# Score pieces on two PSUM banks, the state's sum in one round, and moved splits, in a block of recurrent and attention layers

## The chip, the cores and the metric

The kernel runs on one core of one Trainium2 chip. The metric is the device time of one execution in microseconds (us). PE is TensorE (matmuls, with its weight loads in the row PEld), DVE is VectorE, ACT is ScalarE, POOL is GpSimd, SP is SyncE, whose queue issues nearly every DMA of this kernel.

## The reference

The input goes through a first block (a gated delta rule, a dilated attention, a feed-forward stage), which the change does not touch, and through two layers of a second block, over 1,280 tokens (256 of context and 1,024 others). Each layer of the second block computes, cut to what matters here:

```python
proj = h @ w_in                                # ..., queries, keys, values, gates
# a linear recurrence in both directions over chunks of 64 tokens, 6 heads of 64:
#   state' = decay * (state + what the chunk adds, itself a function of state)
ys = rwkv_bidir(...)
# attention, 6 query heads on 2 key heads, each query over all 1280 keys
s  = q @ k.T ;  p = softmax(s) ;  ya = p @ v
# neighbourhood attention, 4 heads: 8 or 9 rows of 64 keys, with a bias, and the 256 of context
yn = softmax(concat(q @ k_nb.T + bias, q @ k_ctx.T)) @ v
x  = layer_norm(ALPHA * x + gate * (concat(ys, ya, yn) * gates) @ w_out)
```

## The kernel before

A layer of the second block has three stages. In the **projections** (`project`, `project_rest`) the columns of `w_in2` are loaded by `Dense.load` in slabs of 256: each half slab of 128 columns is a DMA into `wraw`, then `split` makes an fp32r high part on ACT (`whi`, L148) and a low part as the difference (`wlo`, L149; POOL unless another engine is named). A product is three matmuls for each of eight slices of the inner dimension (L208 to L210). `Dense.chan` keeps the weights stationary and streams up to 512 tokens. `Dense.tok` keeps 128 tokens stationary and streams the weights' columns. Two places for `whi` and `wlo` take turns, so a slab waits for the matmuls of the slab before last.

Values are 384 columns: for each of ten token tiles one `tok` of 256 columns and one of 128 into the same bank, a copy to `nv` and a DMA. These loads stand at the end of `project_rest`, behind `qk_norm`, whose ten tiles PE, DVE, ACT and POOL work on together with `factors`, the recurrence's inputs.

The **rounds** follow: attention and recurrence, recorded in an order written out by `Rounds`. Every piece of work is a generator that yields a phase and a lag. A round runs through its phases in the order of `PHASES`, and in each phase through all generators that wait for it and whose lag is over. B and Q exist only in odd rounds. The order of recording is the order of instructions on PE, DVE, ACT and POOL; SP's order is left to the framework's scheduler. Per round there is at most:

- scores: a piece of up to 512 columns, as a pair of matmuls (L648) into tag "a", which is one PSUM bank. DVE adds the bias, writes `S` and takes the maximum (L652). Of four pieces three have phase F0 of a round each, and the fourth F2 of the third one's round. When a row of 1,280, 768, 832 or 256 columns is complete, `soft` has ACT take the exponential (L607) and DVE the reciprocal.
- values: one group of four transposes (F1, L684) into tag "t", an ACT copy to `PT` (L688), and the products of the group before (V, L703). Four buffers `S` bound how far scores run ahead.
- the scan of the recurrence: for each of ten block pairs and two chunks, `pw` (L1726), an ACT copy to `W`, `pw` again (L1740), an ACT copy to `SA`, then `py` (L1749, closed by L1767) for the output and `pc` (L1732, closed by L1755) for the new state, which two DVE operations (L1763) scale into `SK`. The chunk takes four rounds.
- `prep`: products and a triangular inverse (`tri_inverse2`) for each of 30 triples, three at a time. It sends a small matrix to DRAM and reads it back spread over partitions (`wR<-wD`), then does 30 small POOL operations (L396, L398).
- `end`: the normalisation of a finished group, and the DMA of `y` to `ydr` (L1818).

Layer 1 computes no output for the context, and so has fewer attention jobs. In `finish`, last, each token tile is read back from `ydr`, gated, multiplied by `w_out` and normalised. Its pools and the recurrence's lie on the same side of SBUF.

Of the kernel before, what the change touches and what calls it, by code (L numbers as in the profile page):

```python
# [27 lines left out]
FIRST = {**ATT, "mm": FULL[0], "r": FULL[0], "o": FULL[1], "g": FULL[5], "h": [(6, 0, 256), (6, 256, 512)],  # L28
         "s": FULL[7]}
SECOND = {**ATT, "mm": FULL[0], "g": FULL[5], "h": [(6, 0, 256), (5, 0, 256), (6, 0, 256), (5, 256, 512)],  # L30
          "z": [(6, 256, 384), (6, 384, 512)], "s": [(7, 0, 384)], "c": [(1, 0, 384)]}


class Consts:
# [139 lines left out]
class Dense:  # L174
# [3 lines left out]
    def __init__(self, k, pools, rpool, width=256, raws=1):  # L178
        self.k, self.pools, self.rpool, self.width, self.raws, self.turn = k, pools, rpool, width, raws, 0

    def load(self, segs, kt=8, width=None, pool=None):

        width = width or self.width
        nc = self.k.nc
        i = "" if pool else self.turn % len(self.pools)
        if not pool:
            self.turn += 1
            pool = self.pools[i]
        hi = pool.tile([128, kt, width], F32R, tag=f"whi{i}", name="whi", bufs=1)
        lo = pool.tile([128, kt, width], F32R, tag=f"wlo{i}", name="wlo", bufs=1)  # L190
        for ap, c0 in segs:
            n = ap.shape[1]
            rw = min(128, width) if kt == 8 else width // 2
            for a in range(0, n, rw):
                m = min(rw, n - a)
                raw = self.rpool.tile([128, kt, rw], F32, tag="wraw", name="wraw", bufs=self.raws)[:, :, :m]
                nc.sync.dma_start(raw, ap[:, a:a + m].rearrange("(k p) n -> p k n", p=128))
                c = slice(c0 + a, c0 + a + m)
                self.k.split(hi[:, :, c], lo[:, :, c], raw)
        return hi, lo  # L200

    def product(self, p, lhs, rhs):
# [159 lines left out]
def tri_inverse2(k, pool, At, out, ticket):  # L362

    nc = k.nc
# [21 lines left out]
    x = new("X16", (128, 4, 16))  # L386
    nc.gpsimd.tensor_copy(x, k.c("eye16")[:, None, :].to_broadcast([128, 4, 16]))
    tmp = new("Y16", (128, 4, 16))
    yield "-", 3
    for i in range(15):  # L390
        if i in (3, 6, 10):
            yield "-", 1
# [191 lines left out]
def attend_rounds(k, rounds, wk, jobs, width, bufs):  # L584
# [18 lines left out]
        state.more = False  # L603

    def soft(s, mx, total, job):
        yield "-", 1
        nc.scalar.activation(s[:, :total], s[:, :total], AF.Exp, bias=mx[:, 5:6], accum_out=mx[:, 6:7])  # L607
        yield "-", 1
        nc.vector.reciprocal(mx[:, 7:8], mx[:, 6:7])
        job[2].append((s, mx))  # L610
        if len(job[2]) == 2:
            ready.append(job)

    def scores():
        count = 0
        while state.more or loaded:
            if not loaded:
                yield "-", 1
                continue
            segs, blocks, out = loaded.pop(0)  # L620
            job = [blocks, out, []]
            total = sum(n for n, _, _ in segs)
            for h in range(2):
                while live[0] >= bufs:
                    yield "-", 1
                live[0] += 1
                s = wk.tile([128, width], F32, tag="S", name="S", bufs=bufs)
                mx = wk.tile([128, 8], F32, tag="mx", name="mx", bufs=8)

                pieces, c0 = [], 0  # L630
                for n0, score, bias in segs:
                    a = 0
                    while a < n0:
                        n = min(n0 - a, 512 - c0 % 512)
                        if c0 % 512 == 0:
                            pieces.append([])
                        pieces[-1].append((c0, a, n, score, bias))
                        a += n
                        c0 += n
                j = 0  # L640
                for piece in pieces:
                    count += 1
                    yield ("F2", 0) if count % 4 == 0 else ("F0", 1)
                    p = k.bank([128, 512], "a")
                    for c0, a, n, score, bias in piece:
                        ops = score(h, a, n)
                        for i, (lhsT, rhs) in enumerate(ops):
                            nc.tensor.matmul(p[:, c0 % 512:c0 % 512 + n], lhsT=lhsT, rhs=rhs, start=i == 0,  # L648
                                             stop=i == len(ops) - 1)
                    for c0, a, n, score, bias in piece:  # L650
                        b = bias(h)[:, a:a + n] if bias is not None else k.zero.to_broadcast([128, n])
                        nc.vector.tensor_tensor_reduce(out=s[:, c0:c0 + n], in0=p[:, c0 % 512:c0 % 512 + n], in1=b, scale=1.0,  # L652
                                                       scalar=-3.0e38, op0=ALU.add, op1=ALU.max, accum_out=mx[:, j:j + 1])
                        j += 1
                if j > 1:
                    nc.vector.tensor_reduce(mx[:, 5:6], mx[:, :j], AX.X, ALU.max, negate=True)  # L656
                else:
                    nc.vector.tensor_scalar(mx[:, 5:6], mx[:, 0:1], -1.0, None, ALU.mult)
                rounds.add(soft(s, mx, total, job))
            state.scored += 1  # L660

# [744 lines left out]
def project_rest(k, I, l, last, hp, dn, hT, L):  # L1406
# [24 lines left out]
        next(side, None)  # L1431
        next(side, None)

    wq = [dn.load([(W[:, 1280 + g * 256:1536 + g * 256], 0)]) for g in range(2)]
    for t in range(10):
        p = k.bank([128, 512], "mm")
        for g in range(2):
# [1 line left out]
        qk_norm(k, hp, p, t, last, L)  # L1439
        next(side, None)  # L1440
        next(side, None)
    wv = [dn.load([(W[:, 1792:2048], 0)]), dn.load([(W[:, 2048:2176], 0)])]
    for t in range(10):
        p = k.bank([128, 512], "mm")[:, :384]
        dn.tok(wv[0], 0, 256, hT, t * 128, p=p[:, :256])
        dn.tok(wv[1], 0, 128, hT, t * 128, p=p[:, 256:])
        nv = hp.tile([128, 384], F32, tag="nv", name="nv", bufs=2)
        k.copy(nv, p)
        nc.sync.dma_start(L.nv[:, t], nv)
        next(side, None)  # L1450
    for _ in side:
        pass

# [134 lines left out]
class Rounds:  # L1588
# [1 line left out]

    PHASES = (("-", "F0", "F1", "F2", "V"), ("-", "F0", "F1", "F2", "V", "B", "Q"))

    def __init__(self):
        self.live, self.r = [], 0
# [27 lines left out]
def rwkv(k, rounds, wk, l, last, L):  # L1624
# [86 lines left out]
    def scan():  # L1711
        for s in range(10):
# [6 lines left out]
            for ci in range(2):  # L1719
# [4 lines left out]
                for pr, d, u in units:  # L1724
                    for h in range(2):
                        nc.tensor.matmul(pw[HS[h], pr, d], lhsT=g[h][:, pr, u, 0:64], rhs=sk[h][:, pr, 0, u],  # L1726
                                         start=True, stop=True)
                if new:
                    pc = k.bank([128, 3, 2, 64], "c")
                    for pr, d, u in units:  # L1730
                        for h in range(2):
                            nc.tensor.matmul(pc[HS[h], pr, d], lhsT=sk[h][:, pr, 1, u], rhs=sk[h][:, pr, 0, u],  # L1732
                                             start=(pr, d) == (0, 0), stop=False, skip_group_check=True)
                W = t1("W", (128, 3, 2, 64))
                nc.scalar.copy(W, pw)
                yield "B", 1
# [4 lines left out]
                                         start=True, stop=True)  # L1741
                SA = t1("SA", (128, 3, 2, 64), 2)
                nc.scalar.activation(SA, pw, AF.Copy, scale=-1.0)
                yield "V", 1
                if want(s):
                    py = k.bank([128, 3, 2, 64], "s")
                    for pr, d, u in units:
                        for h in range(2):
                            nc.tensor.matmul(py[HS[h], pr, d], lhsT=sk[h][:, pr, 0, u], rhs=g[h][:, pr, u, 64:128],  # L1749
                                             start=(pr, d) == (0, 0), stop=False, skip_group_check=True)  # L1750
                yield "B", 0
                if new:
# [36 lines left out]
    def end(o, pr, g):  # L1789
# [17 lines left out]
        nc.vector.tensor_copy(rs, pm)  # L1807
        yield "-", 1
        k.rsqrt(rs, rs, 1.0 / 64, 64e-5)
        yield "V", 1  # L1810
        pm = k.bank([128, 2, 128], "mm")
        for b in range(2):
            for h in range(2):
# [417 lines left out]
```

## Time and profile before

| | us |
|---|---|
| median of 2 runs | 4754.6 |
| the two runs | 4746.42, 4762.78 |
| the profiled execution | 4747.42 |
| its span, first to last instruction | 4745.4 |
| layer 0's rounds, about | 2235 to 3065 |
| layer 1's rounds, about | 3815 to 4650 |

The granted clock has the mean 0.904 over the span; 1.0 stands for 2.4 GHz and 0.5 for 1.2 GHz. A matmul's row includes its passage through the array, so rows of one run overlap, and what PE can do in a stretch is read from the distance of starts. A wait is PE's idle time in front of an instruction, put down to what released it.

### The profile page before, as it was taken

Reading aid. Unit: us, or ns where it says so; the run is one execution under the profiler, and the core shown is the slowest. Engines: PE = TensorE matmul, PEld = TensorE weight load, DVE = VectorE, ACT = ScalarE, POOL = GpSimd, SP = SyncE. Lnnn points to the kernel's source line nnn. Section 1 sums busy time; section 2 is a strip of 40 time slices with the busy share of each in tenths; the row PEclk is TensorE's granted clock in tenths of the full one; section 3 lists DMA queues with packets and bytes.
Section 4 is the critical chain, followed back from the end, with each engine's and each line's share of the span. In section 5 each row is a group of like instructions: output and inputs, shape, how many; then the busy total and the mean of one; then the engine's idle time right before and its main releaser. Section 6 shows DMA issues by size and latency. Waiting matters only on the chain. (4 is left out here: it accounts for less than half of the span.)

```text
span 4745.4 us, 92034 instructions
## 1 busy us (share of the span) xinstructions
PE 4060.8 (86%) x37134; PEld 3294.0 (69%) x37134; DVE 2142.5 (45%) x4637; ACT 1479.2 (31%) x2843; POOL 1861.8 (39%) x3279
## 2 busy tenths in 40 slices
PE   8999998989999898985778887788988758887888
PEld 6767778777888687775556666567877736666667
DVE  5533333693121543561344444455446334444445
ACT  4244443311111312321334433332133124433342
POOL 2433343432222524562243443235257332434423
PEclk9999999999999899987879987789998868988889
DMA  3433224452111324533222223433355232223343
GB/s 108 135 114 90 82 81 140 147 160 67 45 49 45 120 86 127 199 116 92 56 71 63 68 73 80 126 104 109 106 181 174 80 96 53 68 63 81 83 116 123
DMA packets 525403, 472.01 MB, mean 99 GB/s; under 512 B 67344, under 2 KB 447792, under 8 KB 524848
## 3 DMA queue, kind: packets, MB, share of 16 engines
q1 hardware_dynamic: 524976, 466.13, 33.2%
q8 instruction: 291, 4.77, 0.4%
q14 instruction: 136, 1.11, 0.1%
HBM read 335.54 MB, written 130.43 MB: 98 GB/s over the span
## 5 line engine op out<-in xcount | busy, mean ns | idle before, releaser
L149 POOL TENSOR_TENSOR wlo<-wraw,whi 128x1024 fp32r<-128x1024 f32 (+3 forms) x188 | 451.5, 2414 | 737.4 <-ACT whi L148 647.3
L396 POOL TENSOR_TENSOR wY<-wR,wX 128x60 f32<-128x60 f32 (+1 forms) x900 | 229.2, 255 | 385.5 <-DMA wR<-wD 324.2
L652 DVE CUSTOM_DVE_ANT_0 S<-bank,zero 128x256 f32<-128x256 f32 (+1 forms) x372 | 208.2, 560 | 289.4 <-PE bank L648 287.8
L148 ACT CAST whi<-wraw 128x1024 fp32r<-128x1024 f32 (+3 forms) x188 | 182.8, 999 | 470.1 <-PE bank L209 172.1
L688 ACT COPY PT<-bank 128x512 f32<-128x512 f32 x346 | 202.2, 585 | 347.9 <-PE bank L684 346.0
L210 PE MATMUL bank<-h2T,wlo 128*128 128x512 f32 x704 | 278.3, 397 | 0.0
L209 PE MATMUL bank<-h2T,whi 128*128 128x512 f32 x704 | 277.9, 395 | 0.0
L208 PE MATMUL bank<-h2T,whi 128*128 128x512 f32 x704 | 275.7, 394 | 0.3 <-ACT h2T L744 0.3
L684 PE MATMUL bank<-cst,S 128*128 128x128 f32 (+1 forms) x1416 | 255.2, 308 | 21.6 <-ACT PT L688 15.0
L398 POOL TENSOR_TENSOR wX<-wX,wY 128x60 f32<-128x60 f32 (+1 forms) x900 | 238.2, 265 | 70.5
L703 PE MATMUL bank<-PT,nav 128*64 128x128 f32 (+1 forms) x2832 | 260.8, 309 | 4.3 <-ACT PT L688 3.4
L607 ACT ACTIVATE S<-S,mx 128x1280 f32<-128x1280 f32 (+3 forms) x180 | 202.9, 1127 | 189.0 <-DVE mx L656 183.5
L208 PE MATMUL bank<-whi,yh 128*128 128x256 f32 x832 | 242.6, 292 | 18.4 <-ACT yh L148 14.3
L210 PE MATMUL bank<-whi,yl 128*128 128x256 f32 x832 | 240.4, 289 | 1.9 <-DVE yl L149 1.9
L209 PE MATMUL bank<-wlo,yh 128*128 128x256 f32 x832 | 241.3, 290 | 0.0
L684 PEld LDWEIGHTS bank<-cst,S 128*128 128x128 f32 (+1 forms) x1416 | 180.3, 155 | 70.1 <-ACT PT L688 36.7
L703 PEld LDWEIGHTS bank<-PT,nav 128*64 128x64 f32 (+1 forms) x2832 | 164.7, 149 | 79.6 <-issue 66.5
L208 PE MATMUL bank<-hA,whi 128*128 128x512 f32 (+1 forms) x528 | 197.1, 373 | 25.4 <-ACT fo L126 14.9
L648 PE MATMUL bank<-k1h,qst 128*128 128x512 f32 (+2 forms) x234 | 121.2, 520 | 104.7 <-DVE mx L652 103.3
L375 POOL TENSOR_TENSOR wB<-A,cst 128x256 f32<-128x256 f32 x60 | 44.8, 747 | 407.5 <-DVE A L1687 396.9
L208 PE MATMUL bank<-hT,whi 128*128 128x512 f32 x464 | 189.8, 409 | 9.6 <-ACT sqkv L126 6.7
L209 PE MATMUL bank<-hA,whi 128*128 128x512 f32 (+1 forms) x528 | 196.2, 372 | 0.4 <-POOL hA L149 0.4
(447 smaller groups left out, 11176.3 us busy)
## 6 DMA issues: line engine op xcount, KB each, us to landing
wraw<-in_w_in SPq DMA_DIRECT2D x86, 512.0 KB
wR<-wD SPq DMA_DIRECT2D x60, 512.0 KB
wm<-in_w_mod SPq DMA_DIRECT2D x96, 256.0 KB
X<-R SPq DMA_DIRECT2D x12, 1280.0 KB
G<-gt SPq DMA_DIRECT2D x24, 640.0 KB
bk<-bk SPq DMA_DIRECT2D x24, 640.0 KB
bk<-bk SPq DMA_DIRECT2D x120, 128.0 KB
G<-G SPq DMA_DIRECT2D x240, 64.0 KB
```

Source lines behind the costliest of these rows:

```text
L148: self.nc.scalar.copy(hi, raw)
L149: (eng or self.nc.gpsimd).tensor_tensor(lo, raw, hi.bitcast(F32), ALU.subtract)
L208: nc.tensor.matmul(p, lhsT=lh, rhs=rh, start=kk == 0, stop=False)
L209: nc.tensor.matmul(p, lhsT=lh, rhs=rl, start=False, stop=False)
L210: nc.tensor.matmul(p, lhsT=ll, rhs=rh, start=False, stop=kk == n - 1)
L396: nc.gpsimd.tensor_tensor(t, custom(R, i * 64 + i + 1, [((15 - 2 * i) * 64 + 31 - i, 2), (16, 2), (1, n)]), custom(x, i, [(47 - 2 * i, 2), ...
L398: nc.gpsimd.tensor_tensor(o, o, t, ALU.subtract)
L607: nc.scalar.activation(s[:, :total], s[:, :total], AF.Exp, bias=mx[:, 5:6], accum_out=mx[:, 6:7])
L652: nc.vector.tensor_tensor_reduce(out=s[:, c0:c0 + n], in0=p[:, c0 % 512:c0 % 512 + n], in1=b, scale=1.0, scalar=-3.0e38, op0=ALU.add, op1= ...
L684: nc.tensor.transpose(pt[:rows[i], i], P[h][0][:, c0:c0 + rows[i]], k.ident)
L688: nc.scalar.copy(t[:, :full], pt[:, :full])
L703: nc.tensor.matmul(pv[h * 64:h * 64 + 64, 0], lhsT=V, rhs=t[:V.shape[0], i], start=seen[h] == 1, stop=seen[h] == n)
```

## The change

- Tag "a" has two banks, the one it had and the one in which `pc` lies. Every odd piece is F0 of a new round, and every even one F2 of the same round, so that up to two pieces stand in a round.
- `pc`'s first matmuls move from the round of the first `pw` to a new phase V2, three rounds later, right behind `py` and ahead of B of the same odd round. `py` moves there too, from the round before.
- `soft` runs in a new last phase Z: the exponential at the end of the round in which its row is complete, not at the start of the next.
- `tri_inverse2` waits a round longer before its first POOL operations, and `end` a round longer before its last product.
- The last 128 value columns are a slab of their own, projected by `chan` over 256, 512 and 512 tokens; each result is copied, transposed back in 128-token blocks, copied and written.
- The low parts of the slabs for queries, keys and values (seven 128x1024 pieces a layer) are made on DVE, not on POOL.

```diff
-          "z": [(6, 256, 384), (6, 384, 512)], "s": [(7, 0, 384)], "c": [(1, 0, 384)]}
+          "z": [(6, 256, 384), (6, 384, 512)], "s": [(7, 0, 384)], "c": [(1, 0, 384)], "a": FULL[2] + FULL[1]}
...
     tmp = new("Y16", (128, 4, 16))
-    yield "-", 3
+    yield "-", 4
...
     def soft(s, mx, total, job):
-        yield "-", 1
+        yield "Z", 0
         nc.scalar.activation(s[:, :total], s[:, :total], AF.Exp, bias=mx[:, 5:6], accum_out=mx[:, 6:7])
-        yield "-", 1
+        yield "Z", 1
...
-                    yield ("F2", 0) if count % 4 == 0 else ("F0", 1)
+                    yield ("F0", 1) if count % 2 else ("F2", 0)
...
-    wq = [dn.load([(W[:, 1280 + g * 256:1536 + g * 256], 0)]) for g in range(2)]
+    wq = [dn.load([(W[:, 1280 + g * 256:1536 + g * 256], 0)], eng=nc.vector) for g in range(2)]
...
-    wv = [dn.load([(W[:, 1792:2048], 0)]), dn.load([(W[:, 2048:2176], 0)])]
+    w = dn.load([(W[:, 1792:2048], 0)], eng=nc.vector)
     for t in range(10):
-        p = k.bank([128, 512], "mm")[:, :384]
-        dn.tok(wv[0], 0, 256, hT, t * 128, p=p[:, :256])
-        dn.tok(wv[1], 0, 128, hT, t * 128, p=p[:, 256:])
-        nv = hp.tile([128, 384], F32, tag="nv", name="nv", bufs=2)
+        p = k.bank([128, 512], "mm")[:, :256]
+        dn.tok(w, 0, 256, hT, t * 128, p=p)
+        nv = hp.tile([128, 256], F32, tag="nv", name="nv", bufs=2)
         k.copy(nv, p)
-        nc.sync.dma_start(L.nv[:, t], nv)
+        nc.sync.dma_start(L.nv[:, t, 0:256], nv)
         next(side, None)
+    w = dn.load([(W[:, 2048:2176], 0)], eng=nc.vector)
+
+    def turn(p, t0, n):
+        o = slot("fo")[:, :n]
+        k.copy(o, p)
+        q = k.bank([128, 512], "r")[:, :n]
+        for b in range(0, n, 128):
+            nc.tensor.transpose(q[:, b:b + 128], o[:, b:b + 128], k.ident)
+        v = slot("fth")[:, :n]
+        k.copy(v, q)
+        nc.sync.dma_start(L.nv[:, t0 // 128:(t0 + n) // 128, 256:384], v.rearrange("p (b c) -> p b c", c=128))
+
+    dn.chan(w, 0, hT, SEG, turn)
...
-    PHASES = (("-", "F0", "F1", "F2", "V"), ("-", "F0", "F1", "F2", "V", "B", "Q"))
+    PHASES = (("-", "F0", "F1", "F2", "V", "Z"), ("-", "F0", "F1", "F2", "V", "V2", "B", "Q", "Z"))
...
-                if new:
-                    pc = k.bank([128, 3, 2, 64], "c")
-                    for pr, d, u in units:
...
-                yield "V", 1
+
+                yield "V2", 1
                 if want(s):
                     py = k.bank([128, 3, 2, 64], "s")
...
+                if new:
+                    pc = k.bank([128, 3, 2, 64], "c")
+                    for pr, d, u in units:
...
         k.rsqrt(rs, rs, 1.0 / 64, 64e-5)
-        yield "V", 1
+        yield "V", 2
```

The order of PE's instructions in layer 0, before, in three rounds of attention with little of the recurrence; L648 are pieces of scores, L684 transposes, L703 products, `bank_73` the one bank of tag "a":

```order
L648 MATMUL bank_73<-k0h,qst 128x256
L648 MATMUL bank_73<-k0l,qst 128x256
L684 MATMUL bank_74<-cst,S 128x128 x4
L648 MATMUL bank_73<-k1h,qst 128x512
L648 MATMUL bank_73<-k1l,qst 128x512
L703 MATMUL bank_75<-PT,nav 64x128 x4
L648 MATMUL bank_73<-k1h,qst 128x512
L648 MATMUL bank_73<-k1l,qst 128x512
L684 MATMUL bank_74<-cst,S 128x128 x4
L703 MATMUL bank_75<-PT,nav 64x128 x4
```

The same kind of place now; `bank_72` is the second bank:

```order
L648 MATMUL bank_72<-k0h,qst 128x512
L648 MATMUL bank_72<-k0l,qst 128x512
L684 MATMUL bank_74<-cst,S 128x128 x4
L648 MATMUL bank_73<-k0h,qst 128x512
L648 MATMUL bank_73<-k0l,qst 128x512
L703 MATMUL bank_75<-PT,nav 64x128 x4
L648 MATMUL bank_72<-k0h,qst 128x256
L648 MATMUL bank_72<-k0l,qst 128x256
L684 MATMUL bank_74<-cst,S 128x128 x4
L648 MATMUL bank_73<-k1h,qst 128x512
```

Neighbouring pieces lie in different banks, and every round has two of them around its transposes. In layer 0 the first piece of a round is in `bank_72`, in layer 1 the second.

PE around a state's sum in layer 0, now; L1756 is `py`, L1762 the first matmuls of `pc`, L1768 and L1780 what closes the two (before, L1732 stood behind the first `pw`, L1726, some three rounds ahead of L1755):

```order
L648 MATMUL bank_72<-k1h,qst 128x512
L648 MATMUL bank_72<-k1l,qst 128x512
L684 MATMUL bank_74<-cst,S 128x128 x4
L648 MATMUL bank_73<-k1h,qst 128x256
L648 MATMUL bank_73<-k1l,qst 128x256
L703 MATMUL bank_75<-PT,nav 64x128 x4
L1756 MATMUL bank_78<-G_16412,SK_16408 64x64
...
L1762 MATMUL bank_72<-SK_16408 64x64
...
L1768 MATMUL bank_72<-SA,betok_16418 64x64 x12
L1780 MATMUL bank_78<-AB_16416,SA 64x64 x12
```

The sum opens and closes within one round, in a bank that a piece of the same round has just used.

SP's DMAs where layer 1's rounds end, before (`ydr<-y` is the recurrence's last output, `wraw<-in_w_out` the first weights of `finish`, `ydr<-rsum` an attention output):

```order
L1818 DMA ydr_28671<-y 128x2x128 x3
L1845 DMA qraw<-nqk_28667 64x128 x4
L197 DMA wraw<-in_w_out 128x8x128 x2
L1952 DMA gaterows<-gr_84 128x1024 x2
L1845 DMA qraw<-nqk_28667 64x128 x4
L1879 DMA ydr_28671<-rsum 128x128
```

Now:

```order
L1892 DMA ydr_28528<-rsum 128x128
L1831 DMA ydr_28528<-y 128x2x128 x3
L1982 DMA lx<-x1d 128x1024
L1985 DMA lnrows<-in_ln_g 128x1024
L1986 DMA lnrows<-in_ln_b 128x1024
L197 DMA wraw<-in_w_out 128x8x128 x2
```

Before, four attention outputs follow the first output weights. Now attention is over, and the recurrence ends last.

## Rows read from the trace of the kernel before

**Rows 1.** Page, part 1: busy us (share of the span), engine by engine
```profile
PE 4060.8 (86%) x37134; PEld 3294.0 (69%) x37134; DVE 2142.5 (45%) x4637; ACT 1479.2 (31%) x2843; POOL 1861.8 (39%) x3279
```

**Rows 2.** Windows: length, busy us (instructions) PE PEld DVE ACT POOL, PEclk, DMA share, GB/s
```profile
2240.00:3060.00 820.00, 638.79 (x10188) 487.81 (x10189) 353.02 (x1120) 317.84 (x672) 307.16 (x978) 0.83 0.30 77
...
3000.00:3040.00 40.00, 19.71 (x123) 12.45 (x122) 20.92 (x42) 18.73 (x36) 16.21 (x8) 0.63 0.75 199
...
3820.00:4640.00 820.00, 650.45 (x10183) 497.38 (x10183) 347.44 (x1105) 318.45 (x650) 318.17 (x1019) 0.86 0.31 79
```

**Rows 3.** PE's waits, layer 0's rounds: us in total, times, longest
```profile
PE bank L648 <- DVE mx L652: 72.1, 72, 3.7
PE bank L144 <- POOL wU L400: 29.8, 5, 12.0
PE bank L648 <- DVE qst L1872: 12.2, 4, 9.1
```

**Rows 4.** PE's waits, layer 1's rounds
```profile
PE bank L648 <- DVE mx L652: 76.8, 76, 4.0
PE bank L144 <- POOL wU L400: 22.2, 7, 10.9
```

**Rows 5.** Timeline of PE: start, us; one piece of scores behind another
```profile
2478.78 0.50 PE L648 MATMUL bank<-k0h,qst 128*128 128x512 f32 x1
2479.11 0.40 PE L648 MATMUL bank<-k0l,qst 128*128 128x512 f32 x1
2480.30 0.50 PE L648 MATMUL bank<-k0h,qst 128*128 128x512 f32 x1 [0.79 <-DVE mx L652]
```

**Rows 6.** Groups by line, layer 0's rounds: count, busy us, mean ns, idle before
```profile
L684 PE MATMUL bank<-cst,S 128*128 128x128 f32 x632 | 110.4, 302 | 5.2 <-ACT PT L688 3.6
...
L652 DVE CUSTOM_DVE_ANT_0 S<-bank,zero 128x512 f32<-128x512 f32 x96 | 66.2, 690 | 77.2 <-PE bank L648 77.0
...
L1763 DVE TENSOR_TENSOR SK<-bank,wc 64x384 f32<-64x384 f32 x38 | 21.1, 555 | 34.4 <-PE bank L1755 34.1
```

**Rows 7.** Tile S, whole run: count, ns min/median/max, first and last start
```profile
L684 PE MATMUL bank<-cst,S x1416: 270/273/476, 2249.0 to 4654.8; 128*128 128x128 f32 x173, 128*64 128x128 f32 x4
```

**Rows 8.** Timeline of PE, value projection, layer 0: first matmul of each group
```profile
2176.11 0.22 PE L208 MATMUL bank<-whi,hA 128*128 128x128 f32 x1
...
2178.74 0.34 PE L208 MATMUL bank<-whi,hA 128*128 128x256 f32 x1
...
2181.67 0.22 PE L208 MATMUL bank<-whi,hA 128*128 128x128 f32 x1
```

**Rows 9.** Timeline of PE: first matmuls of two 512-column groups, weights stationary
```profile
1880.51 0.39 PE L208 MATMUL bank<-hA,whi 128*128 128x512 f32 x1
...
1886.42 0.40 PE L208 MATMUL bank<-hA,whi 128*128 128x512 f32 x1
```

**Rows 10.** PE's waits, layer 0's projections, 1790 to 2235 us
```profile
PE bank L208 <- DVE xg L1551: 14.0, 5, 9.4
```

**Rows 11.** A 128x1024 DVE operation on two SBUF tensors: ns min/median/max
```profile
L1992 DVE TENSOR_TENSOR lx<-lx,lnrows x18: 1205/1226/2693, 3161.9 to 4740.5; 128x1024 f32<-128x1024 f32 x18
```

**Rows 12.** Tile W and PE's timeline: one link of the scan's chain
```profile
L1735 ACT COPY W<-bank x40: 462/480/482, 2344.2 to 4549.8; 128x384 f32<-128x384 f32 x40
...
2702.76 0.87 PE L1749 MATMUL bank<-G,SK 128*64 128x64 f32 x24
```

**Rows 13.** Line L1816, then timelines of SP, POOL, PE: end of layer 1
```profile
L1816 DVE SCALAR_TENSOR_TENSOR y<-y,gng,bank x27: 479/480/482, 2416.8 to 4574.8; 128x256 f32<-128x256 f32 x27
...
4578.76 1.22 SPq L197 DMA_DIRECT2D wraw<-in_w_out  x2
...
4601.80 2.38 POOL L149 TENSOR_TENSOR wlo<-wraw,whi 128x1024 fp32r<-128x1024 f32 x1
...
4659.20 0.58 PE L208 MATMUL bank<-whi,yh 128*128 128x256 f32 x1 [2.77 <-DVE ltmp L1983]
```

More of the change, by code (lines that the diff above doesn't have):

```diff
@@ L179, in __init__, with load @@
         self.k, self.pools, self.rpool, self.width, self.raws, self.turn = k, pools, rpool, width, raws, 0
-    def load(self, segs, kt=8, width=None, pool=None):
+    def load(self, segs, kt=8, width=None, pool=None, eng=None):
         width = width or self.width
@@ L198, in load @@
                 c = slice(c0 + a, c0 + a + m)
-                self.k.split(hi[:, :, c], lo[:, :, c], raw)
+                self.k.split(hi[:, :, c], lo[:, :, c], raw, eng)
         return hi, lo
@@ L1727, in scan @@
                                          start=True, stop=True)
-                if new:
-                    pc = k.bank([128, 3, 2, 64], "c")
-                    for pr, d, u in units:
-                        for h in range(2):
-                            nc.tensor.matmul(pc[HS[h], pr, d], lhsT=sk[h][:, pr, 1, u], rhs=sk[h][:, pr, 0, u],
-                                             start=(pr, d) == (0, 0), stop=False, skip_group_check=True)
                 W = t1("W", (128, 3, 2, 64))
@@ L1749, in scan @@
                             nc.tensor.matmul(py[HS[h], pr, d], lhsT=sk[h][:, pr, 0, u], rhs=g[h][:, pr, u, 64:128],
+                                             start=(pr, d) == (0, 0), stop=False, skip_group_check=True)
+                if new:
+                    pc = k.bank([128, 3, 2, 64], "c")
+                    for pr, d, u in units:
+                        for h in range(2):
+                            nc.tensor.matmul(pc[HS[h], pr, d], lhsT=sk[h][:, pr, 1, u], rhs=sk[h][:, pr, 0, u],
                                              start=(pr, d) == (0, 0), stop=False, skip_group_check=True)
```

## The prediction

> **What bounds the kernel now.** I read the page first: PE is busy for 86% of the span and no other engine for half of it [rows 1], so the question is where PE is not busy. The windows answer that: in 820 us of layer 0's rounds PE is busy for 638.8 us, and in as much of layer 1's for 650.5 us, with a granted clock of 0.83 and 0.86 [rows 2]. That is 181 and 170 us of idle time in stretches that make up a third of the kernel, and nearly all that the change touches lies there. The waits of PE say what ends this idle time. By far the largest entry in both layers is a matmul of scores that waits for DVE to take the previous piece's maximum: 72.1 us in 72 waits, and 76.8 us in 76 [rows 3, 4], together 148.9 us. The timeline shows one: a pair of matmuls starts at 2478.78, the next pair at 2480.30 after 0.79 us of idle PE [rows 5]. Tag "a" has one bank, and the eviction that frees it takes 690 ns of DVE [rows 6]. DVE itself waits for PE there (77.0 us before that group, [rows 6]): it is idle, not late. So the two engines take turns on one bank.
>
> The second loss is the clock. A transpose of `S` has a median of 273 ns and a maximum of 476 [rows 7], and the mean in layer 0's rounds is 302 [rows 6], 10.6% above the median. If all of PE's work there is stretched alike, the low level (1.2 GHz) costs 638.8 x (1 - 273/302) = 61 us in layer 0, and about as much in layer 1.
>
> **The change, part by part.** The sum is made against the profiled execution, 4747.4 us; the median of the runs is 4754.6, 7 us above it, well inside the spread of the two runs.
>
> *Two banks for scores.* Two pieces a round now lie in different banks, and a bank comes round again a round later. Stepping both tables of phases through the jobs gives 320 and 284 rounds before, 271 and 254 now (layers 0 and 1): an average round is 830/320 = 2.6 us, so 0.69 us of eviction has ended when its bank is wanted. Some waits stay, where DVE has the inverse's work in front of the eviction; the longest are 3.7 and 4.0 us [rows 3, 4]. I leave 20 us of the 148.9: **-129**, between -149 and -75.
>
> *The clock.* With 65 us less idle time in each layer, part of the stretch goes too. I take 40% of the 61 us, the share of the idle time that goes (65 + 12 of 181): **-50** for both layers, between 0 and -122.
>
> *Drains.* Before, attention ran to round 319 in layer 0 and the recurrence's last output came in round 252; the switch to the last pair of heads fell outside it, and a window of 40 us there has PE busy for 19.7 us at a clock of 0.63 [rows 2]. Now attention ends in round 270, and that switch falls among the recurrence's rounds. Of the 20 us I take **-12**, between -20 and 0.
>
> *Layer 1's end.* There attention now ends in round 234 and the recurrence, unchanged in its rounds, in 253, so that the last 19 rounds have next to nothing in them but the scan's own chain. One link of it is some 0.9 us of PE and 0.48 us of ACT [rows 12]. Two chunks of three such links and the state's two operations of 555 ns [rows 6] are 2 x (3 x 1.4 + 1.1) = 11 us, and the normalisation behind them is about as long: 20 us, which attention covered before. Behind it come the output weights, which use the recurrence's memory. Before, the recurrence's last group was done at 4574.8, the weights were asked for at 4578.8, the fourth low part was made by 4601.8 + 2.4 = 4604.2, and the first output matmul ran at 4659.2 [rows 13]: 25 us of loading under attention's tail. Now nothing covers it, though SP has less in between. **+45** in all, between +25 and +60. In layer 0 attention still ends 17 rounds after the recurrence, some 45 us, which covers the loading.
>
> *The state's sum.* `pc` and `py` are the same matmuls two rounds later or earlier; SA is ready two rounds ahead of them. But the bank is shared: in layer 0 the next round's first piece waits for the two operations that scale the state, in layer 1 `pc` waits for the eviction of a piece just made. Between the two stand 24 matmuls or more, 0.87 us [rows 12], against 1.1 us and 0.69 us of DVE [rows 6]. I take 0.25 us for each of 76 sums: **+19**, between 0 and +60.
>
> *Values.* A token tile costs 24 matmuls of 128 columns, 2178.74 - 2176.11 = 2.63 us, and 24 of 256, 2.93 us [rows 8]: half the columns at nearly the same price. Ten times 2.63 us go. What comes is 2.93 us for the 256 tokens, twice 5.91 us for 512 [rows 9], and ten transposes at no more than 0.27 us [rows 7]: 17.5 us. That is 8.8 us less for a layer, **-18** for both, between -23 and 0 (copy, transpose, copy and DMA behind the last product hold up the rounds' first loads by two or three us).
>
> *Splits on DVE.* Seven low parts a layer leave POOL, at 2.4 us each [rows 13], and cost DVE 1.2 us each [rows 11]. PE waits for DVE's `qk_norm` for 14.0 us there already [rows 10], and a low part that waits for its DMA now holds up DVE, where it held up POOL and, through `qss`, DVE. I take 0, between -10 and +20. The nearest row of the same shape on DVE runs between 1205 and 2693 ns [rows 11]. The Trainium skill (SBUF — State Buffer, Who interferes with whom) says that a DVE instruction with two SBUF inputs contends with POOL's reads, which is in keeping with that row; at 2.7 us a piece the layer would pay 19 us of DVE in place of 8, and the sum would be some 20 us higher.
>
> *Lags.* A round more ahead of the inverse's POOL work and of `end`'s last product costs nothing in rounds: the phase behind the inverse's loop exists in odd rounds only, and it falls in the same one. PE's waits for that loop (29.8 and 22.2 us, [rows 3, 4]) stay as they are: they come from the DRAM round trip, which takes as long as before. The exponential moves by less than a round on ACT.
>
> The sum is -129 - 50 - 12 + 45 + 19 - 18 = -145: 4602, rounded to **4600 us**.
>
> **The rivals.**
>
> *The clock stays where it is* (10%). PE still stops for the inverse's POOL work, for the keys and for the state [rows 3, 4]. If those stops and not the short ones hold the clock down, the term of -50 goes: 4652. For it: in the drained window the clock is 0.63 [rows 2], and long waits remain. Against it: the clock is 0.86 where PE is busy for 650 of 820 us, so it follows the whole stretch's load, not those few stops alone. The Trainium skill (TensorE: Matmul & The Clock Gate, A second HAM failure mode: psum-queue depth-cycling) has a kernel that cycles through PSUM banks and whose clock swings all the same, because PE pauses briefly between groups; by that page the time would be this rival's.
>
> *The waits move* (17%). Rounds with two pieces bring DVE two evictions of 0.69 us, and ACT a `PT` copy right behind an exponential. If half of the 148.9 us comes back under other names and the clock does not rise, the time is 4602 + 55 + 50 = 4707, no difference that can be told. For it: DVE's work is not spread evenly, and one bank "t" stays single. Against it: DVE and ACT are busy for 353 and 318 of 820 us [rows 2].
>
> *All of it comes back* (8%). No wait for the bank, no cost of sharing and a full clock: 4602 - 20 - 19 - 72 = 4491.
>
> *The change does not do what it says* (5%). The rounds become fewer and fuller but PE's queue waits as long in each, because the recurrence's chain sets the pace; only the values' -18 is left: 4729. Against it: the recurrence needs 253 rounds either way, and its last group ended 84 us ahead of the first output matmul [rows 13].
>
> *The shared bank makes it slower* (4%). A sum that waits for an eviction, or a piece that waits for the state, holds PE's whole queue and the scan's chain. The price is 76 sums times the wait. The gains without it are 145 + 19 = 164 us, so it decides from 164/76 = 2.2 us a sum, and makes the kernel slower by 2% from (164 + 95)/76 = 3.4 us. Waits of 3.7 and 4.0 us for DVE exist [rows 3, 4], but as the longest of 148 whose mean is 1.0 us.
>
> **The numbers.** The forecast has 56%, with its own range from 4530 to 4660. Two per cent is 95 us, about what a measurement of this kernel can tell from no change; so faster means below 4660. The forecast (54 of its 56), the clock's rival (8 of 10) and the full gain (8) lie there, and 2 of the moved waits' 17: 72%. The rest of these and the case without effect make 24%, slower has 4%. The range from 4510 to 4715 leaves out half of the full gain, the case without effect, the slower one and some of the moved waits: about 2 in 10.
>
> **What would show it.** Right: the wait of scores for DVE falls below 30 us over both layers, PE's idle share in the windows of the rounds falls from 22% to about 15%, and the granted clock there rises to 0.88 or more; layer 0's rounds shorten by 80 us or more, layer 1's by less; first output weights are asked for behind the last `ydr<-y`, with PE nearly idle for 30 to 50 us. Wrong: waits of `pc` (now L1762) or of the score matmuls for the state's scaling in tens of us; new waits of L684 for the `PT` copy; a clock that stays at 0.85; or waits of the projections for DVE that grow by more than 20 us.

## The result, and the profile after

The changed kernel takes 4573.4 us (4569.4 and 4577.4), 0.962 of the time before (95% interval 0.954 to 0.970). A second set of its runs, E5 below, gives 0.9606 (0.9583 to 0.9628), which is 187 us of 4738.5. The forecast was 4600 us, 145 us less than the profiled execution. Direction, size and the likeliest case were right; about 40 us of gain were missing from the sum.

The table splits profiled executions at the first matmul of a layer's projections (L208 with `hA` or `hB`), at its first piece of scores (L648), and at the last instruction. Two executions of the change (this one and E5) differ by up to 9 us in these columns. Block 1, which no kernel here changes, ends between 1613 and 1634 us, so that part is noise.

| us | projections 0 | rounds and finish 0 | projections 1 | rounds and finish 1 |
|---|---|---|---|---|
| before | 607 | 1033 | 564 | 922 |
| after | 592 | 915 | 538 | 895 |
| E5, after once more | 591 | 906 | 539 | 895 |
| E3, one bank | 593 | 1002 | 539 | 960 |
| E7, two banks, former rounds | 591 | 937 | 541 | 861 |
| E2, two banks, former rate | 591 | 923 | 544 | 859 |
| E6, exponential a round later | 591 | 941 | 542 | 874 |
| E8, rate by layer | 595 | 906 | 544 | 852 |
| E1, rounds alone | 604 | 902 | 563 | 887 |

Page, part 1, of the changed kernel, against [rows 1]: PE has 120 us less busy time with nearly the same work.

```profile
PE 3940.7 (86%) x36818; PEld 3236.4 (71%) x36818; DVE 2151.8 (47%) x4657; ACT 1465.3 (32%) x2849; POOL 1826.1 (40%) x3265
```

Windows of the rounds of both layers and of the end of layer 1 (columns as in [rows 2]):

```profile
2240.00:2980.00 740.00, 616.91 (x10480) 490.23 (x10482) 361.35 (x1218) 331.03 (x718) 286.16 (x955) 0.90 0.31 79
3680.00:4390.00 710.00, 572.65 (x9660) 454.87 (x9660) 323.77 (x1071) 301.44 (x635) 279.52 (x982) 0.88 0.30 73
4393.50:4442.60 49.10, 19.69 (x368) 15.56 (x366) 9.16 (x24) 7.02 (x13) 8.24 (x8) 0.70 0.43 121
```

The clock rose from 0.83 to 0.90 in layer 0 and from 0.86 to 0.88 in layer 1 [rows 2]. PE idles for 123 of 740 us and 137 of 710, 18% together against 21% before: less idle, but more than the 15% forecast.

PE's waits, layer 0's rounds, against [rows 3]:

```profile
PE bank L144 <- POOL wU L400: 34.1, 9, 15.1
PE bank L684 <- ACT PT L688: 10.5, 11, 2.6
PE bank L703 <- ACT PT L688: 10.2, 9, 1.8
...
PE bank L648 <- DVE mx L652: 7.1, 7, 1.7
```

And layer 1's, against [rows 4]:

```profile
PE bank L144 <- POOL wU L400: 37.8, 9, 12.6
PE bank L684 <- ACT PT L688: 16.6, 18, 2.6
PE bank L648 <- DVE mx L652: 13.7, 7, 2.7
...
PE bank L1762 <- DVE mx L652: 7.1, 7, 2.5
```

The wait for the bank, 148.9 us before, is 20.8. The largest entry is now the wait for the inverse's POOL work, 71.9 us where it was 52.0. The waits for the `PT` copy have grown too: those of L684 alone were 5.4 and 5.8 us before. The timeline of PE shows the removed wait's place, against [rows 5]:

```profile
2476.34 0.50 PE L648 MATMUL bank<-k0h,qst 128*128 128x512 f32 x1
2476.67 0.40 PE L648 MATMUL bank<-k0l,qst 128*128 128x512 f32 x1
2476.91 0.60 PE L684 MATMUL bank<-cst,S 128*128 128x128 f32 x4
2477.26 0.48 PE L648 MATMUL bank<-k0h,qst 128*128 128x512 f32 x1
2477.58 0.40 PE L648 MATMUL bank<-k0l,qst 128*128 128x512 f32 x1
2477.91 0.66 PE L703 MATMUL bank<-PT,nav 128*64 128x128 f32 x8
2478.49 0.39 PE L648 MATMUL bank<-k0h,qst 128*128 128x256 f32 x1
```

Pairs start 0.92 and 1.23 us apart, with transposes and products between them and no idle time; before, two pairs with nothing between started 1.52 us apart.

Timelines of PE and then SP at the end of layer 1: attention's last group, the recurrence's last matmuls, the first output product; then the recurrence's last output and the first output weights.

```profile
4393.50 0.44 PE L707 MATMUL bank<-cst,mx 128*64 128x128 f32 x4
...
4422.11 1.12 PE L1827 MATMUL bank<-cst,hrs 128*64 128x128 f32 x8 [0.73 <-DVE y L1829]
4442.64 0.58 PE L208 MATMUL bank<-whi,yh 128*128 128x256 f32 x1 [19.40 <-ACT yh L148]
...
4420.66 4.07 SPq L1831 DMA_DIRECT2D ydr<-y  x3
...
4426.26 1.52 SPq L197 DMA_DIRECT2D wraw<-in_w_out  x2
```

Between attention's end and the first output product lie 49 us in which PE is busy for 19.7 at a clock of 0.70: the bare end that the prediction described.

### The profile page after: what moved, and what is told of

Read it like the earlier page. It is cut to its first block, busy times and chain, and to the rows that moved or that the text cites. A ratio compares the mean times of both kernels' runs of the same rounds, so it can differ in the third digit from the quotient of the medians.

```text
span 4567.6 us, 91476 instructions
## 1 busy us (share of the span) xinstructions
PE 3940.7 (86%) x36818; PEld 3236.4 (71%) x36818; DVE 2151.8 (47%) x4657; ACT 1465.3 (32%) x2849; POOL 1826.1 (40%) x3265
## 5 line engine op out<-in xcount | busy, mean ns | idle before, releaser
L149 POOL TENSOR_TENSOR wlo<-wraw,whi 128x1024 fp32r<-128x1024 f32 (+3 forms) x174 | 417.4, 2412 | 712.6 <-ACT whi L148 654.7
L208 PE MATMUL bank<-whi,yh 128*128 128x256 f32 x832 | 243.9, 294 | 50.3 <-ACT yh L148 34.2
L208 PE MATMUL bank<-h2T,whi 128*128 128x512 f32 x704 | 276.0, 395 | 0.3 <-ACT h2T L744 0.3
L684 PE MATMUL bank<-cst,S 128*128 128x128 f32 (+1 forms) x1416 | 246.5, 300 | 33.0 <-ACT PT L688 27.1
L703 PE MATMUL bank<-PT,nav 128*64 128x128 f32 (+1 forms) x2832 | 253.6, 303 | 19.7 <-ACT PT L688 16.9
L684 PEld LDWEIGHTS bank<-cst,S 128*128 128x128 f32 (+1 forms) x1416 | 176.6, 151 | 83.8 <-ACT PT L688 46.3
L703 PEld LDWEIGHTS bank<-PT,nav 128*64 128x64 f32 (+1 forms) x2832 | 160.3, 146 | 94.0 <-issue 58.1
L208 PE MATMUL bank<-hA,whi 128*128 128x512 f32 (+1 forms) x552 | 205.9, 373 | 24.1 <-ACT fo L126 15.1
L209 PE MATMUL bank<-hA,whi 128*128 128x512 f32 (+1 forms) x552 | 205.1, 372 | 0.4 <-POOL hA L149 0.4
L208 PEld LDWEIGHTS bank<-whi,yh 128*128 128x128 f32 x832 | 165.9, 200 | 53.0 <-ACT yh L148 35.8
L210 PE MATMUL bank<-hA,wlo 128*128 128x512 f32 (+1 forms) x552 | 203.1, 368 | 0.0
```

The lines of the kernel that those rows point to most:

```text
L149: (eng or self.nc.gpsimd).tensor_tensor(lo, raw, hi.bitcast(F32), ALU.subtract)
L208: nc.tensor.matmul(p, lhsT=lh, rhs=rh, start=kk == 0, stop=False)
L209: nc.tensor.matmul(p, lhsT=lh, rhs=rl, start=False, stop=False)
L210: nc.tensor.matmul(p, lhsT=ll, rhs=rh, start=False, stop=kk == n - 1)
L684: nc.tensor.transpose(pt[:rows[i], i], P[h][0][:, c0:c0 + rows[i]], k.ident)
L703: nc.tensor.matmul(pv[h * 64:h * 64 + 64, 0], lhsT=V, rhs=t[:V.shape[0], i], start=seen[h] == 1, stop=seen[h] == n)
```

## The experiments

Ratios are to the kernel before on the same chip; differences between experiments are differences of ratios times 4740 us, with both intervals combined. Edits are to the changed kernel unless said otherwise.

**E3: one bank.**

```diff
-          "z": [(6, 256, 384), (6, 384, 512)], "s": [(7, 0, 384)], "c": [(1, 0, 384)], "a": FULL[2] + FULL[1]}
+          "z": [(6, 256, 384), (6, 384, 512)], "s": [(7, 0, 384)], "c": [(1, 0, 384)]}
```

> The change with one bank for the scores' pieces (the former one), still up to two pieces a round; the state's sum keeps its own bank. Theory A (the bank): every second piece waits for the eviction of the piece before, with only four transposes between, so the waits of scores for DVE are back at 120 to 200 us over both layers and the time is 4680 to 4760 us. Theory B (fuller rounds): 4580 to 4630 us.

4718.1 us, ratio 0.9948 (0.9932 to 0.9964): without the second bank the rest of the change is worth 25 us, and the bank 162 us (149 to 175; E3 against E5). Its waits, layer 0 and then layer 1:

```profile
PE bank L648 <- DVE mx L652: 74.7, 104, 3.0
PE bank L144 <- POOL wU L400: 28.3, 6, 14.1
...
PE bank L648 <- DVE mx L652: 73.0, 94, 3.5
```

In E5, the same code with two banks, the same two entries are:

```profile
PE bank L648 <- DVE mx L652: 7.8, 8, 1.7
...
PE bank L648 <- DVE mx L652: 14.0, 9, 2.7
```

Theory A holds. The windows of rounds and finish tell what the bank does, first E3, layers 0 and 1:

```profile
2214.00:3216.00 1002.00, 805.18 (x11531) 640.50 (x11532) 469.15 (x1355) 374.07 (x783) 401.84 (x1091) 0.87 0.31 84
3755.00:4715.00 960.00, 736.90 (x10856) 580.64 (x10856) 415.35 (x1198) 334.29 (x678) 359.54 (x1050) 0.86 0.30 80
```

then E5:

```profile
2209.00:3115.00 906.00, 741.66 (x11534) 612.51 (x11534) 464.03 (x1355) 371.35 (x783) 400.61 (x1091) 0.91 0.34 92
3653.00:4548.00 895.00, 699.10 (x10856) 573.06 (x10856) 409.83 (x1198) 333.38 (x678) 357.99 (x1050) 0.87 0.32 86
```

The waits for the bank fall by 126 us (147.7 to 21.8), but PE's idle time only by 60 (420 to 360). The other 101 us are busy time of the same instructions (1542 to 1441).

**E2: two banks at the former rate.**

```diff
-                    yield ("F0", 1) if count % 2 else ("F2", 0)
+                    yield ("F2", 0) if count % 4 == 0 else ("F0", 1)
```

> The change with the former rate of pieces: two banks that take turns, but four pieces in three rounds (320 and 284 rounds again). Theory A (the bank is what PE waited for): the waits of scores for DVE stay below 30 us over both layers though the rounds are many, and attention covers layer 1's end again; 4540 to 4600 us. Theory B (what helped is that rounds are fewer and fuller, so that a round's waits for other engines are paid less often): most of the gain in the rounds is lost, 4660 to 4720 us, with the waits for DVE gone or not.

4532.3 us, ratio 0.9553 (0.9522 to 0.9583): 25 us faster than the change (7 to 43). Its rounds are 302 and 266, not 320 and 284 as the expectation says, because the exponential stays at the round's end. The waits for the bank are 25.8 us over both layers, as theory A has it; the time lies just below its range. Fuller rounds are not what helped.

**E7: two banks and the former rounds.** E2's edit, and the exponential and the reciprocal back in the next rounds:

```diff
-        yield "Z", 0
+        yield "-", 1
...
-                    yield ("F0", 1) if count % 2 else ("F2", 0)
+                    yield ("F2", 0) if count % 4 == 0 else ("F0", 1)
```

> The second bank with the rounds of the kernel before: four pieces in three rounds and the exponential in the next round, so attention's last rounds are 319 and 283 again. Theory A (the bank alone takes the waits away, and the number of rounds costs nothing by itself): 4520 to 4560 us, like the run with two banks at the former rate (ratio 0.955), whose rounds were 302 and 266. Theory B (each of the 36 rounds more costs a microsecond or so): 4560 to 4600 us.

4549.5 us, ratio 0.9598 (0.9573 to 0.9624): with 320 and 284 rounds it takes as long as the change (4 us less, give or take 16). Theory A holds. By the table the change's rounds gain 31 us in layer 0 against E7 and lose 34 in layer 1.

**E6: the exponential in the next round.** The lines of `soft` alone.

```diff
-        yield "Z", 0
+        yield "-", 1
...
-        yield "Z", 1
+        yield "-", 1
```

> The change with the exponential and the reciprocal of a row back at the start of the next round and of the one after; all else as changed. Attention then ends in rounds 277 and 241, not 270 and 234. Theory A (the prediction: moving the exponential by less than a round costs and gives nothing): the time of the change within 10 us. Theory B (the exponential at a round's start stands in front of that round's copy of the transposes on ACT, 1.1 us, so that PE's products and transposes wait for the copy, and the buffers of rows come free later): 20 to 40 us slower than the change, with PE's waits for the copies up from 44 us to over 60 over both layers.

4562.4 us, ratio 0.9625 (0.9603 to 0.9648): 9 us slower than the change, give or take 15, so nothing that can be told. The table shows two effects of opposite sign: layer 0 takes 35 us more than in E5, layer 1 21 us less. PE's waits for the copy into `PT` rise in layer 0 (22 to 40 us) and fall in layer 1 (24 to 16). That is theory B's mechanism in layer 0 alone, and both layers together stay below its 60 us.

**E1: the rounds alone.** The splits for queries, keys and values are on POOL, and all value columns are projected token by token, as before.

```diff
-    wq = [dn.load([(W[:, 1280 + g * 256:1536 + g * 256], 0)], eng=nc.vector) for g in range(2)]
+    wq = [dn.load([(W[:, 1280 + g * 256:1536 + g * 256], 0)]) for g in range(2)]
...
-    w = dn.load([(W[:, 1792:2048], 0)], eng=nc.vector)
+    wv = [dn.load([(W[:, 1792:2048], 0)]), dn.load([(W[:, 2048:2176], 0)])]
...
-    dn.chan(w, 0, hT, SEG, turn)
```

> The change's rounds alone: the value projection, its order and the engine of the splits are those of the kernel before. Theory A (what the stages of the two traces say): the projections, which got 15 and 26 us shorter in the two layers, give 41 us of the 181, so this kernel takes about 4573 + 41 = 4614 us (4600 to 4625). Theory B (the prediction's terms: values -18, splits 0): it takes about 4573 + 18 = 4591 us (4585 to 4598), and the remaining 23 us of the projections' gain are a matter of how the rounds and the projections meet.

4575.3 us, ratio 0.965 (0.9626 to 0.9673): 21 us more than E5, give or take 15. Theory A's 41 us are out, and theory B's 18 within reach, though the projections of this trace are 36 us longer than E5's.

**E11: the projections alone.** E1's edit the other way round, on the kernel before.

```diff
-    wv = [dn.load([(W[:, 1792:2048], 0)]), dn.load([(W[:, 2048:2176], 0)])]
+    w = dn.load([(W[:, 1792:2048], 0)], eng=nc.vector)
...
+    dn.chan(w, 0, hT, SEG, turn)
```

> The kernel before with the changed projections alone (last value columns channel-major, seven low parts a layer on DVE). Theory A (the prediction's -18 us, or the 34 us by which the projections of the two traces differ): ratio 0.993 to 0.996. Theory B (given back in the rounds, since the first of them wait for the recurrence's inputs anyway): 0.998 to 1.001.

4707.0 us, ratio 0.9939 (0.9918 to 0.9961): 29 us less than before, give or take 10. Theory A holds, nearer its larger figure.

**E4: splits on POOL.**

```diff
-    w = dn.load([(W[:, 1792:2048], 0)], eng=nc.vector)
+    w = dn.load([(W[:, 1792:2048], 0)])
...
-    w = dn.load([(W[:, 2048:2176], 0)], eng=nc.vector)
+    w = dn.load([(W[:, 2048:2176], 0)])
```

The two slabs of queries and keys likewise.

> The change with the seven low parts a layer for queries, keys and values made on POOL again. Theory A (the prediction's term of 0 for the splits): the same time within 10 us, 4563 to 4583 us. Theory B (the projections gained 41 us where the values explain 18, and the splits the rest): 4590 to 4600 us.

4562.8 us, ratio 0.9632 (0.9603 to 0.966): 12 us more than E5, give or take 17. It doesn't tell the theories apart; the projections of the two traces differ by 7 us.

**E5: the change again.**

> The change itself once more, for a ratio from more runs and for a comparison with the runs beside it. Theory A: the projections' part (values and splits) is worth 15 us or less, as the kernel with the rounds alone says (ratio 0.965, 0.963 to 0.967): a ratio of 0.961 to 0.965. Theory B: it is worth the 36 us by which the projections of that kernel's trace were longer: 0.956 to 0.960.

4553.2 us, ratio 0.9606 (0.9583 to 0.9628). The ratio lies just below theory A's range, and its interval meets both; with E1 and E11 the projections come to 20 to 30 us.

**E8: a rate for each layer**, with E4's edit:

```diff
-                    yield ("F0", 1) if count % 2 else ("F2", 0)
+                    yield ("F2", 0) if count % rounds.per == 0 else ("F0", 1)
...
             rounds = Rounds()
+            rounds.per = 4 if last else 2
```

> A candidate to beat both: up to two pieces a round in layer 0, four pieces in three rounds in layer 1 (attention's last rounds 270 and 265, the recurrence's 253 in both), and the splits back on POOL. Theory A (layer 1's bare end is what the change lost: its rounds and finish took 859.2 us at the former rate against 894.7, while layer 0's took 923.0 against 914.8): 8 us less than the run with the former rate in both layers, ratio 0.950 to 0.955. Theory B (the former rate is better in itself, and layer 0 gains from it too once disturbances are averaged): slower than that run, ratio 0.956 to 0.960.

4519.7 us, ratio 0.955 (0.9523 to 0.9576), 27 us faster than the change, give or take 16: the fastest kernel here, if not told apart from E2. The ratio is the upper edge of theory A's range, and its interval reaches theory B's; layer 1, which takes 44 us less than in E5 while layer 0 takes the same, speaks for theory A. Timelines of its SP and PE at the end of layer 1:

```profile
4376.34 3.00 SPq L1831 DMA_DIRECT2D ydr<-y  x3
4380.34 1.05 SPq L197 DMA_DIRECT2D wraw<-in_w_out  x2
...
4394.78 0.44 PE L707 MATMUL bank<-cst,mx 128*64 128x128 f32 x4
4395.15 0.39 PE L208 MATMUL bank<-whi,yh 128*128 128x256 f32 x1
```

The recurrence ends first, the weights load under attention's last groups, and the first product follows attention's last at once. In the change the same two rows lie 49 us apart.

**E10: three pieces in two rounds in layer 1.** E8 with

```diff
-            rounds.per = 4 if last else 2
+            rounds.per = 3 if last else 2
```

> The same candidate, but in layer 1 three pieces in two rounds: attention's last round is 252 there, beside the recurrence's 253. Theory A (layer 1 loses by the bare end alone): the near-empty rounds behind attention's end are gone, about 30 us of the 44 by which the change's layer 1 is longer, while the output weights' loading, some 18 us, stays bare; layer 1's rounds and finish take about 866 us, ratio 0.957 to 0.960. Theory B (a rate lower than two a round helps by itself, as PE's idle time is spread): nearly all of the 44 us, 850 to 857 us, ratio 0.953 to 0.956.

4528.0 us, ratio 0.956 (0.9538 to 0.9582), in reach of both theories. Layer 1 speaks for theory A: 867.1 us. Attention's and the recurrence's last rounds meet, and the load alone stays bare (SP, then PE):

```profile
4398.26 3.93 SPq L1831 DMA_DIRECT2D ydr<-y  x3
4403.71 1.21 SPq L197 DMA_DIRECT2D wraw<-in_w_out  x2
...
4396.03 0.44 PE L707 MATMUL bank<-cst,mx 128*64 128x128 f32 x4
...
4419.86 0.58 PE L208 MATMUL bank<-whi,yh 128*128 128x256 f32 x1 [19.11 <-ACT yh L148]
```

From attention's last row to the first output product it is 24 us, against 49 in the change. By layer 1's times, 28 of the 44 us that the change loses there against E8 are near-empty rounds and 16 the load. That split is rough: it compares single executions, and the one traced here took 20 us more than the median of its four. In the medians E8 and E10 are 5 us apart, give or take 16.

**E9: triples started two rounds apart.** E8 with

```diff
-TICKETS, STAGGER = 3, 4
+TICKETS, STAGGER = 3, 2
```

> The candidate with a rate for each layer, and the three triples of a block pair started two rounds apart in place of four: the recurrence's last round is 249 in place of 253, attention's stay at 270 and 265. Theory A (the end of layer 1 is covered already, and the inverse waits for its DRAM round trip): no difference that can be told, ratio 0.952 to 0.958. Theory B (the three triples' POOL work, 30 operations of 0.26 us each, now stands close together and PE waits for it): PE's waits for the inverse's POOL work rise from 73 us to 95 or more, ratio 0.959 to 0.963.

4580.5 us, ratio 0.9662 (0.9645 to 0.9679): 53 us slower than E8, more than either theory has. The wait for the inverse's POOL work rises to 102.7 us, as theory B says, and beside it stands one that neither names. Its waits in layer 0:

```profile
PE bank L144 <- POOL wU L400: 48.0, 10, 21.2
PE bank L144 <- DVE G L1703: 44.3, 18, 3.9
```

The transposes of `flips` now wait for DVE's masks `G`, 85.5 us over both layers, where the change has two such waits of 2 us in each layer's projections. The distance of four rounds is worth keeping.

## Why the prediction was right, and where its terms were off

**Two banks, the clock and the shared bank** were put at -129, -50 and +19, -160 together. E3 against E5 measures 162 us. The ledger of the wait was right (149 to 21 us). But two steps behind it were off and cancelled. First, I let nearly all of the removed wait become time. PE's idle time fell by 60 us only, because other waits grew (E3 to E5, both layers): POOL's inverse from 49 to 69 us, the `PT` copies from 28 to 46, the output weights' splits from 8 to 16, together 46 of the 66 us that came back. The rival of moving waits was right on that mechanism, with about half of the wait coming back. Second, the busy time of the same matmuls fell by 101 us, twice what I put down for the clock. If all of E3's busy time scales with the granted clock (0.87 to 0.91 and 0.86 to 0.87), 805 x (1 - 0.87/0.91) + 737 x (1 - 0.86/0.87) = 44 us of it are the clock. Counting the rows of both traces one by one, each up to the next row's start, by line, shape and level of the clock, gives an estimate of 49 us for the clock. Another 24 us are rows right in front of a stop, 512 in E3 and 348 in E5: at the full clock a transpose of `S` counts 273 ns there and 122 where the next row follows at once. The other 28 us are rows that start further apart without a stop, and why they do stays open. So the sum of these terms came out by luck.

The rival that the clock stays where it is fell: 0.83 to 0.90 in layer 0, and by the bank alone 0.87 to 0.91 (E3, E5). The Trainium skill (TensorE: Matmul & The Clock Gate, A second HAM failure mode: psum-queue depth-cycling) had pointed to it, with a kernel whose clock swings while it cycles through banks; here the clock rose, though in layer 1, where the longer waits remain, by no more than 0.02. My measure of the clock was poor, though. The transposes of `S` have a mean of 297 ns in layer 0's rounds now, against 302 [rows 6], a small part of what the granted clock gained.

```profile
L684 PE MATMUL bank<-cst,S 128*128 128x128 f32 x712 | 121.4, 297 | 10.7 <-ACT PT L688 9.3
```

The sharing of the bank cost less than I had put down: 7.1 us of `pc` behind an eviction in layer 1, no such wait in layer 0, and pieces that wait for the state's scaling only for 2.8 us in all. I had put 19.

**Drains**, -12: the table gives 31 us in layer 0 for the change's rounds, with one bank (before against E3) as with two (E7 against E5). The term was too small by 19 us, the largest miss, but these 31 us aren't shown to be drains. I had priced one drained window of 40 us and not the rest of attention's tail behind the recurrence, where PE's idle time falls from 27 us (E7) to 5 (E5). E6, however, which keeps the fuller rounds and has 10 us of idle time in that tail, takes as long in layer 0 as E7. With two banks four of the kernels cross the two parts of the change (rounds and finish, us, each from one execution):

| rate of pieces | exponential | layer 0 | layer 1 |
|---|---|---|---|
| former (E7) | next round | 937 | 861 |
| former (E2) | end of round | 923 | 859 |
| two a round (E6) | next round | 941 | 874 |
| two a round (E5) | end of round | 906 | 895 |

In layer 0 fuller rounds gain 17 us with the earlier exponential and nothing without it. So the step that failed along with the drains is the lag of the exponential, which I had put at 0 and which is worth 14 to 35 us there.

**Layer 1's end**, +45: 39 us (before against E3), 34 (E7 against E5), 44 (E8 against E5). The size agrees, but E6, with the exponential a round later, has 13 us (against E7), so not all of it is the bare end; and the reading behind it was wrong. I took 4659.2 us for the first output matmul of the kernel before [rows 13]; it was only the first behind an idle gap. The first ran 62 us earlier, under attention, as PE's timeline of the kernel before shows:

```profile
4597.24 0.41 PE L208 MATMUL bank<-whi,yh 128*128 128x256 f32 x1
```

So attention's tail covered a quarter of `finish` as well as the loading. That quarter is PE work that moved out of the rounds and left them shorter. Nothing in the prediction weighed this, so that the sum still held is luck.

**Values and splits**, -18 and 0: 21 us (E1) and 29 (E11) together. Whether the splits share in that isn't told by E4. In layer 0 a low part on DVE takes 1234 ns, as put down; in layer 1 the mean is 1493:

```profile
L149 DVE TENSOR_TENSOR wlo<-wraw,whi 128x1024 fp32r<-128x1024 f32 x7 | 8.4, 1234 | 9.9 <-ACT whi L148 9.9
...
L149 DVE TENSOR_TENSOR wlo<-wraw,whi 128x1024 fp32r<-128x1024 f32 x7 | 10.5, 1493 | 8.4 <-ACT whi L148 8.3
```

The dearer figure of 2.7 us is met, but rarely: two of layer 1's seven took 1.79 and 2.55 us. The second of them ran beside a POOL operation of 2.1 us (`kd<-kd,kd`, L1542) that reads SBUF. That agrees with the Trainium skill's rule on shared ports (SBUF — State Buffer, Who interferes with whom), and it costs 2 us in all, where 2.7 us a piece would have made it some 20.

**Lags**, 0: for the exponential the sum can't be told from 0 (E6), but only as the difference of 35 us gained in layer 0 and 21 lost in layer 1. Why layer 1 loses stays open. The recurrence ends last there in both kernels, and in E6 it ends 22 us sooner (730 us behind the layer's first scores, against 752 in E5); attention ends 14 us sooner too, though it has seven rounds more. The two other lags have no run of their own. PE's waits for the inverse's POOL work, which I had left at 52 us, are 71.9; with one bank (E3) they are 49, so the rise goes with the second bank and not with the lag.

In all: -162 for the bank, -31 and +39 for the rounds (exponential included), -21 to -29 for the projections, which makes -175 to -183 against 187 measured (176 to 198). The missing gain of the forecast is the 19 us of layer 0's rounds, the end's 6 and the projections' 3 to 11; what is left is within the noise.

## What to carry to other kernels

Where a matmul waits for the eviction of the same bank, give the tag a second bank first and leave the order alone: with the former rounds (E7) it gave, beside the 20 to 30 us of the projections, the whole gain of the change, and fuller rounds on top only moved time from one layer to the other. A faster stream pays only while it is the one that ends last; look at what its tail covered before, and slow it where another chain ends later. The sum of a wait in the ledger isn't the gain: about half of it came back under other names, and the busy time fell by twice what the clock was put at.

## What was not expected of the hardware

The busy time of an unchanged set of 22,390 matmuls fell by 101 us, 7%, when 126 us of short waits between them went (E3 to E5). Of what the stops cost, more stood in PE's busy time than in its idle time, which fell by 60 us; about half of the busy part is the clock, by the count above. The Trainium skill (Perfetto Trace Analysis, Optimization Strategy) says that one gap that repeats on a busy engine can mean that there is not enough SBUF or PSUM for the next tile. The trace agrees: 198 such waits in E3 are 17 with one bank more, and the time that goes is 162 us, more than the 126 us of the gaps.
